# Latent attention: where the softmax rows are divided by their sums

## The chip, the cores and the metric

The kernel runs on one core of one Trainium2 chip. The metric is the device time of one launch in microseconds (us). The kernel before takes 4326.44 us, the median of three runs (4323.44 to 4328.68).

A core has five engines with an instruction queue each, and every queue is worked through in order: PE (TensorE, matrix products; PEld is its weight load), DVE (VectorE), ACT (ScalarE), POOL (GpSimd) and SP (SyncE, which here only issues transfers). An instruction that waits holds up all that is queued behind it on its engine.

## The reference

One layer of an encoder is applied to two groups of tokens, 256 ("prompt") and 1024 ("sample"), with the same weights. The layer is a mixer (retention beside latent attention), a cross-attention to 256 memory tokens, and a feed-forward part that picks experts by product keys. The change lies in the latent attention alone:

```python
def blk(qc):
    s = (einsum('bqhd,bkhd->bhqk', qc[..., :NOPE], k_nope)
         + einsum('bqhr,bkr->bhqk', qc[..., NOPE:], k_rope))
    p = softmax(s.astype(float32) * scale, axis=-1)
    return einsum('bhqk,bkhd->bqhd', p, v)
```

There are 8 heads with values 64 wide. For every query the output is the sum over the keys of exp(score) times value, divided by the sum of the exp.

## The kernel before

The program goes through these stages in order: the input projection and retention; the latent attention of the first group (256 tokens), whose work is mixed with the keys and values of the memory tokens; the first block of the rest of the layer; the latent attention of the second group (1024 tokens), at 829 to 1119 us of the profiled execution; the other two blocks; the gate tables; and a long dense expert stage. Nearly all products are made in three parts (`mm3`, L176: high by high, high by low, low by high), so a product of 512 columns is three matmuls.

The latent attention is `phase_m`. Its heads are taken two at a time ("a pair", `hp`, four of them). For a pair PE first makes the keys `kt` and the queries `qt`, which ACT and DVE split into a high and a low part. Then come the query tiles of 128 rows, 16 per pair in the second group: four (two heads by two tiles) make a batch, which shares one tile of transposed rows `pT` and one result `po`. The steps of a query tile are

- PE: the scores `sc` (called at L640, recorded under L179 to L181), six matmuls of 512 columns; there are two score buffers
- DVE: the row maximum (L642, recorded under L74)
- ACT: exp of the row into `pe`, with the sum of the row read out behind it (L644); there are two `pe` buffers
- DVE: the reciprocal of the sum, and a copy `r` of it across 64 columns (L646, L647, both under L74)
- PE: eight 128x128 transposes of `pe` (L657) into two PSUM tiles `tr` (there are two), and ACT copies each to `pT` (L658)

Once per batch, in `values`, PE lays the reciprocals out as rows by multiplying each `r` with the identity (L590, four products into the second half of `po`), makes the 16 products of the values with `pT` (L594, first half of `po`), and then ACT copies the second half to `ob` (L597), DVE multiplies the first half with it, ACT and DVE split the result into `oh`, and the ACT queue stores it to `mixT` (L602). `values` of a batch is called (`late`) when the next batch has its first tile under way. Matmuls on float32 data (L590, L594) run as two records each.

The order of the instructions on an engine is not the order of the code: a scheduler places them by its own model of time, and it does so for the whole program. DVE also carries work of later stages in between, a few instructions at a time: the routing of experts (L90) and products of gathered expert rows (`gj`, L90), each placed behind an instruction of the main line.

Of the kernel before, what the change touches and what calls it, by code (L numbers as in the profile page):

```python
# [10 lines left out]
F32 = mybir.dt.float32  # L11
# [4 lines left out]
AF = mybir.ActivationFunctionType  # L16
ALU = mybir.AluOpType
# [4 lines left out]
P = 128  # L22
# [37 lines left out]
def r32(ap):  # L60
    return ap.bitcast(F32)
# [46 lines left out]
class K:  # L108
# [423 lines left out]
    def phase_m(self, sd, g, lw):  # L532
        nc, tc, I = self.nc, self.tc, self.I
        v = self.v
        t0, nt = GROUPS[g]
        Tg = nt * P
        NB = min(Tg, 512)
        with ExitStack() as es:
# [4 lines left out]
            vs = ma.tile([P, nt, 512], F32, name=self.nm("vs"))  # L543
# [36 lines left out]
            po_ = es.enter_context(tc.tile_pool(name="mpo", bufs=1 + g, reuse_waits="tile", space=PSUM))  # L580
            ap = es.enter_context(tc.tile_pool(name="mb", bufs=1, reuse_waits="tile"))
            QG = 2 * P
            late = None

            def values(hp, q0, pTs, rs):

                po = po_.tile([P, 2, QG], F32, tag="po", name=self.nm("po"))
                for j in range(2):
                    for par in range(2):
                        nc.tensor.matmul(po[64 * par:64 * par + 64, 1, j * P:(j + 1) * P], rs[par][j], self.ident, start=True, stop=True)  # L590
                for j in range(nt):
                    for par in range(2):
                        h = 2 * hp + par
                        nc.tensor.matmul(po[64 * par:64 * par + 64, 0, :], vs[:, j, h * 64:(h + 1) * 64], pTs[par][j // 4][:, j % 4, :],  # L594
                                         start=j == 0, stop=j == nt - 1)
                ob = ap.tile([P, QG], F32, tag="ob", name=self.nm("ob"), bufs=2)
                nc.scalar.copy(ob, po[:, 1, :])  # L597
                v.tensor_tensor(ob, po[:, 0, :], ob, ALU.mult)
                oh = [ap.tile([P, QG], F32R, tag=f"oh{i}", name=self.nm("oh"), bufs=1) for i in range(2)]
                self.split(oh[0], oh[1], ob)  # L600
                for i in range(2):
                    nc.scalar.dma_start(sd["mixT"][g][i][:, hp, q0 * P:q0 * P + QG], r32(oh[i]))  # L602
                self.tick(0.1 * nt)

            for hp in range(MH // 2):
                S = kt
                for b in range(0, Tg, NB):
                    ps = pp.tile([P, 512], F32, tag="tr", name=self.nm("tr"))
                    bs = slice(b, b + NB)
                    for k in range(2):  # L610
                        w = [ukv[i][:, k, hp * 128:(hp + 1) * 128] for i in range(2)]
                        self.mm3(ps[:, :NB], w, (cT[0][:, 3 + k, bs], cT[1][:, 3 + k, bs]), k == 0, k == 1)
                    for par, r in ((0, slice(0, 64)), (1, slice(64, 128))):
                        self.split(S[par][0][r, bs], S[par][1][r, bs], ps[r, :NB])
                qts = []
                for par in range(2):
                    h = 2 * hp + par
                    qt = [ap.tile([P, Tg], F32R, tag=f"qt{g}{i}", name=self.nm("qt"), bufs=2) for i in range(2)]
                    for b in range(0, Tg, NB):
                        ps = pp.tile([P, 512], F32, tag="tr", name=self.nm("tr"))  # L620
                        bs = slice(b, b + NB)
                        for k in range(3):
                            self.mm3(ps[:, :NB], [uq[i][:, k, h, :] for i in range(2)], (cT[0][:, k, bs], cT[1][:, k, bs]), k == 0, k == 2)
                        qr = ap.tile([P, NB], F32, tag="qr", name=self.nm("qr"), bufs=1)
                        v.tensor_tensor(qr[:, :NB], ps[:, :NB], tq[par][:, bs], ALU.mult)
                        self.split(qt[0][:, bs], qt[1][:, bs], qr[:, :NB])
                    qts.append(qt)
                for q0 in range(0, nt, 2):
                    pTs, rs = [], []
                    for par in range(2):  # L630
                        qt = qts[par]
                        pT = [ap.tile([P, min(nt, 4), QG], F32, tag=f"pT{g}", name=self.nm("pT"), bufs=4) for _ in range(0, nt, 4)]
                        pTs.append(pT)
                        rs.append([])
                        for t in (q0, q0 + 1):
                            sl = slice(t * P, (t + 1) * P)
                            sp = psc.tile([P, max(Tg, 512)], F32, tag="sc", name=self.nm("sc"))
                            for b in range(0, Tg, NB):
                                bs = slice(b, b + NB)
                                self.mm3(sp[:, bs], (qt[0][:, sl], qt[1][:, sl]), (S[par][0][:, bs], S[par][1][:, bs]), True, True)  # L640
                            st = ap.tile([P, 2], F32, tag="st", name=self.nm("st"), bufs=4)
                            v.tensor_reduce(st[:, 0:1], sp[:, :Tg], AX.X, ALU.max, negate=True)  # L642
                            pe = ap.tile([P, Tg], F32, tag=f"pe{g}", name=self.nm("pe"), bufs=2)
                            nc.scalar.activation(pe[:, :Tg], sp[:, :Tg], AF.Exp, bias=st[:, 0:1], accum_out=st[:, 1:2])  # L644
                            r = ap.tile([P, 64], F32, tag="r64", name=self.nm("r64"), bufs=8)
                            v.reciprocal(st[:, 1:2], st[:, 1:2])  # L646
                            v.tensor_copy(r, st[:, 1:2].broadcast_to([P, 64]))  # L647
                            rs[par].append(r)
                            if late:
                                late()  # L650
                                late = None
                            self.tick(0.11 * nt)
                            for q in range(0, nt, 4):
                                n = min(4, nt - q)
                                ps = pp.tile([P, 512], F32, tag="tr", name=self.nm("tr"))
                                for j in range(n):
                                    nc.tensor.transpose(ps[:, j * P:(j + 1) * P], pe[:, (q + j) * P:(q + j + 1) * P], self.ident)  # L657
                                nc.scalar.copy(pT[q // 4][:, :, (t - q0) * P:(t - q0 + 1) * P], ps[:, :n * P].rearrange("p (a b) -> p a b", b=P))  # L658
                    late = lambda a=(hp, q0, pTs, rs): values(*a)
            late()  # L660


# [702 lines left out]
```

## Time and profile before

| what | us |
|---|---|
| median of three runs | 4326.44 |
| the profiled execution | 4333.59 |
| its span, first to last instruction | 4331.8 |
| PE busy in the span | 3994.1 |
| DVE busy | 3286.3 |
| ACT busy | 1633.1 |
| latent attention of the second group | 829 to 1119 |

A busy matmul is drawn from its start to its modelled end, and consecutive matmuls overlap; what one costs in a stream is read from start to start. The same holds for ACT, where an instruction begins before the one ahead has fully ended.

### The profile page before, as it was taken

The numbers are of one execution on the slowest core, as the hardware profiler recorded it, in microseconds if no ns is written. First come the engines' busy times: TensorE is split into PE (matmuls) and PEld (weight loads), VectorE is DVE, ScalarE is ACT, GpSimd is POOL, SyncE is SP. The second block draws the span as 40 slices with busy tenths as digits, with TensorE's granted clock in tenths as the row PEclk, the third lists the DMA queues.
The fourth block names the chain that finished last, engine by engine and source line by source line (L and its number), as shares of the span: only waits on it lengthen the run. The fifth ranks groups of instructions, "written<-read, shape, count | busy, mean of one in ns | idle before, by whom it ended". The sixth has DMA issues, their size and how long they took to land.

```text
span 4331.8 us, 66450 instructions
## 1 busy us (share of the span) xinstructions
PE 3994.1 (92%) x23202; PEld 3573.5 (82%) x23202; DVE 3286.3 (76%) x7044; ACT 1633.1 (38%) x3568; POOL 2277.9 (53%) x2090
## 2 busy tenths in 40 slices
PE   7999888899899899877899999999999999999997
PEld 7999877667588788766788888898888998888896
DVE  5556422687575697799799888888878788888888
ACT  6333534455443343689322222222222222222222
POOL 2221143012556401468456777776767767676775
PEclk9999999899999999999999999999999999999998
DMA  2112577324778648476876998898988888888887
GB/s 90 37 36 72 203 238 267 105 70 153 235 251 304 211 156 283 147 203 201 285 244 226 332 327 295 321 313 294 320 287 296 305 313 292 305 309 288 316 313 275
DMA packets 489008, 1030.74 MB, mean 238 GB/s; under 512 B 42720, under 2 KB 201952, under 8 KB 488672
## 3 DMA queue, kind: packets, MB, share of 16 engines
q0 software_dynamic: 149536, 545.33, 35.7%
q1 hardware_dynamic: 329200, 470.66, 33.0%
q10 hardware_dynamic: 9936, 10.51, 0.8%
q8 instruction: 182, 2.98, 0.3%
q14 instruction: 154, 1.26, 0.1%
HBM read 901.87 MB, written 124.45 MB: 237 GB/s over the span
## 4 chain that ended last, share of the span: by engine, by line
PE 45%; DVE 17%; issue 7%; DMA 5%; POOL 3%; ACT 2%; SPq 0%; another core or an unknown queue 0%; POOLq 0%; ACTq 0%; DVEq 0%
PE pa L181 6%; PE pa L179 6%; PE pa L180 6%; PE pv L180 5%; PE pv L181 5%; PE pv L179 5%; DVE o L74 4%; PE pj L179 2%; PE pj L181 2%; PE pj L180 2%; DVE gj L90 2%; DVE gps L90 2%; DMA ur<-in_uT 2%; POOL grow L1031 1%; DVE dacc L74 1%
## 5 line engine op out<-in xcount | busy, mean ns | idle before, releaser
L1031 POOL DMA_INDIRECT grow<-in_peer_u,gids x512 | 537.5, 1050 | 784.9 <-DVE gj L90 230.9
L179 PE MATMUL pa<-dxT,uh 128*128 128x384 f32 x2048 | 689.9, 337 | 18.4 <-ACT wr L1199 12.6
L1031 POOL DMA_INDIRECT grow<-in_peer_v,gids x512 | 513.5, 1003 | 350.9 <-DVE gps L90 201.6
L180 PE MATMUL pa<-dxT,uh 128*128 128x384 f32 x2048 | 689.8, 337 | 0.0
L181 PE MATMUL pa<-dxT,ul 128*128 128x384 f32 x2048 | 676.0, 337 | 0.4 <-POOL ul L1188 0.2
L90 DVE SCALAR_TENSOR_TENSOR gps<-grow,ga,gps 128x1024 f32<-128x1024 f32 x512 | 656.5, 1282 | 14.0 <-DMA grow<-in_peer_v,gids 6.2
L179 PE MATMUL pv<-vh,wh 128*128 128x512 f32 x1536 | 605.7, 398 | 44.4 <-DVE dacc L74 39.7
L180 PE MATMUL pv<-vl,wh 128*128 128x512 f32 x1536 | 610.7, 398 | 8.3 <-POOL vl L1216 8.2
L181 PE MATMUL pv<-vh,wl 128*128 128x512 f32 x1536 | 609.3, 397 | 1.8 <-DVE wl L74 1.8
L90 DVE SCALAR_TENSOR_TENSOR gj<-grow,gps 128x1024 bf16<-128x1024 f32 x384 | 466.5, 1215 | 7.9 <-ACT gps L1058 1.6
L74 DVE TENSOR_TENSOR dacc<-pv,dacc 128x1024 f32<-128x1024 f32 x258 | 311.9, 1218 | 152.8 <-PE pv L181 142.1
L212 POOL TENSOR_TENSOR wl<-wraw,wh 128x512 fp32r<-128x512 f32 x180 | 240.2, 1352 | 343.1 <-ACT wh L208 253.4
L179 PEld LDWEIGHTS pa<-dxT,uh 128*128 128x128 f32 x2048 | 386.8, 189 | 33.5 <-ACT wr L1199 14.0
L181 PEld LDWEIGHTS pa<-dxT,ul 128*128 128x128 f32 x2048 | 385.6, 189 | 10.9 <-POOL ul L1188 4.4
L180 PEld LDWEIGHTS pa<-dxT,uh 128*128 128x128 f32 x2048 | 386.8, 189 | 6.4
L179 PEld LDWEIGHTS pv<-vh,wh 128*128 128x128 f32 x1536 | 293.5, 191 | 110.6 <-DVE dacc L74 48.4
L1187 ACT CAST uh<-ur 128x512 fp32r<-128x512 f32 x256 | 158.6, 621 | 584.8 <-DMA ur<-in_uT 539.2
L1188 POOL TENSOR_TENSOR ul<-ur,uh 128x512 fp32r<-128x512 f32 x256 | 333.3, 1306 | 65.1 <-ACT uh L1187 59.1
L1216 POOL TENSOR_TENSOR vl<-vr,vh 128x512 fp32r<-128x512 f32 x256 | 333.2, 1320 | 59.7 <-ACT vh L1215 56.6
L180 PEld LDWEIGHTS pv<-vl,wh 128*128 128x128 f32 x1536 | 293.8, 191 | 66.8 <-POOL vl L1216 12.3
L181 PEld LDWEIGHTS pv<-vh,wl 128*128 128x128 f32 x1536 | 293.3, 191 | 59.3 <-DVE wl L74 2.8
L179 PE MATMUL pj<-act,wh 128*128 128x256 f32 x1088 | 311.1, 295 | 22.4 <-ACT act L173 7.5
(285 smaller groups left out, 9077.6 us busy)
## 6 DMA issues: line engine op xcount, KB each, us to landing
ur<-in_uT SPq DMA_DIRECT2D x256, 256.0 KB
vr<-in_peer_v SPq DMA_DIRECT2D x256, 256.0 KB
G<-st SPq DMA_DIRECT2D x96, 512.0 KB
gt<-G SPq DMA_DIRECT2D x64, 768.0 KB
wraw<-in_peer_wq SPq DMA_DIRECT2D x96, 256.0 KB
wraw<-in_w_out SPq DMA_DIRECT2D x48, 256.0 KB
wraw<-in_ca_wq SPq DMA_DIRECT2D x48, 256.0 KB
x<-ld SPq DMA_DIRECT2D x24, 512.0 KB
```

The costliest lines, as they stand in the source:

```text
L74: r = f(*a, **kw)
L90: r = f(*a, **kw)
L179: mm(ps, a[0], b[0], start=first, stop=False)
L180: mm(ps, a[0], b[1], start=False, stop=False)
L181: self.mm = mm(ps, a[1], b[0], start=False, stop=last).ins
L212: (nc.vector if self.spare and k in self.spare else eng).tensor_tensor(wl[:, :n], raw[:, :n], r32(wh[:, :n]), ALU.subtract)
L1031: nc.gpsimd.indirect_dma_start(out=u, out_offset=None, in_=src, in_offset=bass.IndirectOffsetOnAxis(ap=ids[:, s:s + 1], axis=0))
L1187: nc.scalar.copy(uh, ur)
L1188: nc.gpsimd.tensor_tensor(ul, ur, r32(uh), ALU.subtract)
L1216: nc.gpsimd.tensor_tensor(vl, vr, r32(vh), ALU.subtract)
```

## The change

Each row of exp is multiplied with the reciprocal of its sum on ACT, in place in `pe`, before it is transposed. The tile `r`, its copy on DVE, the products with the identity on PE, the copy to `ob` and the product on DVE are left out, and `po` has one half only; `oh` is split from `po` directly. In the second group that is 64 more ACT instructions of 128x1024, and in the first 16 of 128x256.

```diff
-            def values(hp, q0, pTs, rs):
+            def values(hp, q0, pTs):
-                po = po_.tile([P, 2, QG], F32, tag="po", name=self.nm("po"))
-                for j in range(2):
-                    for par in range(2):
-                        nc.tensor.matmul(po[64 * par:64 * par + 64, 1, j * P:(j + 1) * P], rs[par][j], self.ident, start=True, stop=True)
+                po = po_.tile([P, QG], F32, tag="po", name=self.nm("po"))
...
-                ob = ap.tile([P, QG], F32, tag="ob", name=self.nm("ob"), bufs=2)
-                nc.scalar.copy(ob, po[:, 1, :])
-                v.tensor_tensor(ob, po[:, 0, :], ob, ALU.mult)
-                self.split(oh[0], oh[1], ob)
+                self.split(oh[0], oh[1], po)
...
-                            r = ap.tile([P, 64], F32, tag="r64", name=self.nm("r64"), bufs=8)
                             v.reciprocal(st[:, 1:2], st[:, 1:2])
-                            v.tensor_copy(r, st[:, 1:2].broadcast_to([P, 64]))
-                            rs[par].append(r)
+                            nc.scalar.activation(pe[:, :Tg], pe[:, :Tg], AF.Copy, scale=st[:, 1:2])
```

How ACT's order changes is seen in the middle of a pair of heads of the second group. Before, with `tr` the transposed quarters of a row and `sc` the scores:

```order
L644 ACTIVATE pe_12295,st_12293<-sc_12282,st_12293 128x1024
L658 COPY pT_12251<-tr_12276 128x4x128
L658 COPY pT_12250<-tr_12300 128x4x128
L644 ACTIVATE pe_12323,st_12321<-sc_12314,st_12321 128x1024
L658 COPY pT_12251<-tr_12306 128x4x128
L644 ACTIVATE pe_12383,st_12381<-sc_12374,st_12381 128x1024
L658 COPY pT_12312<-tr_12362 128x4x128
L597 COPY ob_12349<-po_12328 128x256
```

And of the change (L637 is the exp, L639 the new multiplication, L649 the copy):

```order
L637 ACTIVATE pe_11568,st_11566<-sc_11559,st_11566 128x1024
L649 COPY pT_11474<-tr_11545 128x4x128
L649 COPY pT_11475<-tr_11551 128x4x128
L637 ACTIVATE pe_11597,st_11595<-sc_11588,st_11595 128x1024
L639 ACTIVATE pe_11568<-pe_11568,st_11566 128x1024
L639 ACTIVATE pe_11597<-pe_11597,st_11595 128x1024
L649 COPY pT_11557<-tr_11576 128x4x128
L649 COPY pT_11558<-tr_11582 128x4x128
```

Query tiles now go through ACT two by two: both multiplications stand behind the second exp and ahead of the copies.

PE's order at the same place before, where a score product is followed by the transposes of one tile (each `x4` is four transposes) and a product for the sums:

```order
L181 MATMUL sc_12432<-kt_9497,qt_12125 128x512
L590 MATMUL po_12482<-c_ident,r_2541_12325 64x128
L657 MATMUL tr_12392<-c_ident,pe_12383 128x128 x4
L657 MATMUL tr_12398<-c_ident,pe_12383 128x128 x4
L179 MATMUL sc_12464<-kt_9495,qt_12090 128x512
```

And of the change (L648 is the transpose, L591 the product of the values; the score `sc_11559` is complete ahead of these rows, and 13 more value products of the same kind stand between the first two pieces):

```order
L181 MATMUL sc_11559<-kt_9453,qt_11298 128x512
L591 MATMUL po_11493<-pT_11418,vs_9455 64x256
L591 MATMUL po_11493<-pT_11335,vs_9455 64x256
...
L181 MATMUL sc_11588<-kt_9453,qt_11298 128x512
L648 MATMUL tr_11516<-c_ident,pe_11489 128x128 x4
L648 MATMUL tr_11522<-c_ident,pe_11489 128x128 x4
L648 MATMUL tr_11545<-c_ident,pe_11541 128x128 x4
L648 MATMUL tr_11551<-c_ident,pe_11541 128x128 x4
L179 MATMUL sc_11615<-kt_9451,qt_11263 128x512
```

The transposes of two tiles now stand together, behind the scores of the next two tiles, and in every second such group 15 value products stand between those two scores.

## Rows read from the trace of the kernel before

**Rows 1.** The page: span, and busy time of each engine.

```profile
span 4331.8 us, 66450 instructions
PE 3994.1 (92%) x23202; PEld 3573.5 (82%) x23202; DVE 3286.3 (76%) x7044; ACT 1633.1 (38%) x3568; POOL 2277.9 (53%) x2090
```

**Rows 2.** Windows, second group's attention: from:to, length, busy per engine, PE clock, DMA.

```profile
829.00:900.00 71.00, 65.11 (x393) 45.47 (x393) 60.87 (x255) 41.25 (x77) 2.92 (x3) 0.95 0.15 49
900.00:966.00 66.00, 60.92 (x365) 44.99 (x365) 62.80 (x228) 38.21 (x72) 3.13 (x3) 0.97 0.14 44
966.00:1038.00 72.00, 69.88 (x431) 50.19 (x428) 53.03 (x106) 42.48 (x81) 19.14 (x17) 1.00 0.46 140
1038.00:1110.00 72.00, 69.36 (x431) 50.26 (x428) 52.33 (x103) 42.45 (x80) 18.91 (x17) 1.00 0.57 182
```

**Rows 3.** Timeline of ACT, exps at a pair's ends: start, us, instruction.

```profile
1037.88 1.13 ACT L644 ACTIVATE pe<-sc,st 128x1024 f32<-128x1024 f32 x1
1057.79 1.12 ACT L644 ACTIVATE pe<-sc,st 128x1024 f32<-128x1024 f32 x1 [0.51 <-DVE st L74]
1110.59 1.12 ACT L644 ACTIVATE pe<-sc,st 128x1024 f32<-128x1024 f32 x1
```

**Rows 4.** Timeline of PE inside the last pair.

```profile
1067.59 0.44 PE L590 MATMUL po<-c_ident,r 128*64 128x128 f32 x4
1067.96 0.66 PE L657 MATMUL tr<-c_ident,pe 128*128 128x128 f32 x4
1068.37 0.48 PE L179 MATMUL sc<-kt,qt 128*128 128x512 f32 x1
...
1069.85 0.60 PE L657 MATMUL tr<-c_ident,pe 128*128 128x128 f32 x4
...
1072.88 3.62 PE L594 MATMUL po<-pT,vs 128*64 128x256 f32 x31
```

**Rows 5.** Timeline of ACT inside the last pair.

```profile
1069.38 1.11 ACT L644 ACTIVATE pe<-sc,st 128x1024 f32<-128x1024 f32 x1
1070.39 0.19 ACT L644 ACTIVATION_READ_ACCUMULATOR pe<-sc,st 128x1 f32 x1
1070.49 0.59 ACT L658 COPY pT<-tr 128x512 f32<-128x512 f32 x1
...
1079.47 0.59 ACT L658 COPY pT<-tr 128x512 f32<-128x512 f32 x1 [0.31 <-PE tr L657]
...
1079.96 0.59 ACT L658 COPY pT<-tr 128x512 f32<-128x512 f32 x1
```

**Rows 6.** Line groups, 820 to 1120 us: xcount, busy us, mean ns, idle before.

```profile
L590 PE MATMUL po<-c_ident,r 128*64 128x128 f32 x128 | 20.4, 297 | 1.4 <-DVE r L74 1.2
L74 DVE TENSOR_REDUCE st<-sc 128x1 f32<-128x1024 f32 x64 | 77.7, 1216 | 15.2 <-PE sc L181 14.7
L644 ACT ACTIVATE pe<-sc,st 128x1024 f32<-128x1024 f32 x64 | 72.0, 1125 | 14.2 <-DVE st L74 10.1 <-DVE sel L90 1.7 <-DVE r L74 1.7
L597 ACT COPY ob<-po 128x256 f32<-128x256 f32 x16 | 6.0, 372 | 27.8 <-PE po L594 27.7
```

**Rows 7.** Lines 822 and 826, the memory attention's exp and multiplication: ns min/median/max.

```profile
L822 ACT ACTIVATE pe<-s,st x40: 462/475/587, 659.4 to 1585.9; 128x256 f32<-128x256 f32 x40
L826 ACT ACTIVATE pe<-pe,st x40: 491/508/581, 661.4 to 1590.2; 128x256 f32<-128x256 f32 x40
```

**Rows 8.** Windows, after a wait of PE on DVE between two pairs.

```profile
900.00:904.00 4.00, 0.81 (x2) 0.74 (x3) 3.89 (x18) 0.98 (x2) 0.00 (x0) 0.87 0.10 33
904.00:908.00 4.00, 4.00 (x14) 3.11 (x14) 2.61 (x8) 0.87 (x2) 0.00 (x0) 0.70 0.36 98
```

**Rows 9.** Windows, the first group's attention and the stretch behind it.

```profile
480.00:590.00 110.00, 110.00 (x731) 96.44 (x730) 40.67 (x103) 47.94 (x119) 27.79 (x22) 1.00 0.56 184
590.00:630.00 40.00, 27.15 (x113) 20.94 (x112) 11.35 (x17) 14.21 (x27) 15.50 (x13) 0.87 0.89 309
```

More of the change, by code (lines that the diff above doesn't have):

```diff
@@ L593, in values @@
                         h = 2 * hp + par
-                        nc.tensor.matmul(po[64 * par:64 * par + 64, 0, :], vs[:, j, h * 64:(h + 1) * 64], pTs[par][j // 4][:, j % 4, :],
+                        nc.tensor.matmul(po[64 * par:64 * par + 64, :], vs[:, j, h * 64:(h + 1) * 64], pTs[par][j // 4][:, j % 4, :],
                                          start=j == 0, stop=j == nt - 1)
-                ob = ap.tile([P, QG], F32, tag="ob", name=self.nm("ob"), bufs=2)
-                nc.scalar.copy(ob, po[:, 1, :])
-                v.tensor_tensor(ob, po[:, 0, :], ob, ALU.mult)
                 oh = [ap.tile([P, QG], F32R, tag=f"oh{i}", name=self.nm("oh"), bufs=1) for i in range(2)]
-                self.split(oh[0], oh[1], ob)
+                self.split(oh[0], oh[1], po)
                 for i in range(2):
@@ L628, in phase_m @@
                 for q0 in range(0, nt, 2):
-                    pTs, rs = [], []
+                    pTs = []
                     for par in range(2):
@@ L633, in phase_m @@
                         pTs.append(pT)
-                        rs.append([])
                         for t in (q0, q0 + 1):
@@ L658, in phase_m @@
                                 nc.scalar.copy(pT[q // 4][:, :, (t - q0) * P:(t - q0 + 1) * P], ps[:, :n * P].rearrange("p (a b) -> p a b", b=P))
-                    late = lambda a=(hp, q0, pTs, rs): values(*a)
+                    late = lambda a=(hp, q0, pTs): values(*a)
             late()
```

## The prediction, made before the changed kernel was run

> **What bounds the kernel now.** I read the page first: PE is busy 3994 of 4332 us and ACT 1633 [rows 1], so over the whole kernel PE is short and ACT has room. That average decides nothing here, since the change lies in two stretches only. The windows come next. In the second group's attention PE is busy 69.9 and 69.4 of 72 us in the later two stretches, ACT 42.5, DVE 53 and 52 [rows 2]. In the first two DVE is nearly as full as PE (60.9 of 71 and 62.8 of 66), because it carries routing in between. So PE sets the pace in the later half, and PE and DVE by turns in the first.
>
> The third view is the timeline of ACT, for the pace. In the last pair the first exp starts at 1057.79 and the last at 1110.59: 52.8 us for 15 tile steps, 3.52 us a tile or 14.1 us a batch of four. From the last exp of a pair to the first of the next it is 19.9 us (1037.88 to 1057.79) [rows 3]: that is where PE makes the next keys and queries.
>
> The fourth view is the timeline of PE inside that pair, for costs from start to start [rows 4]. Four transposes take 0.41 us (1067.96 to 1068.37), so a tile's eight take 0.82; the six score matmuls take 1.48 (1068.37 to 1069.85); four records of the products with the identity take 0.37 (1067.59 to 1067.96), so the eight of a batch take 0.74; 31 records of the value products take 3.62, so the 32 of a batch take 3.74. A batch on PE is 4 x (1.48 + 0.82) + 3.74 + 0.74 = 13.7 us of the 14.1: PE is the bound by start-to-start costs too.
>
> ACT from start to start [rows 5]: exp with its readout 1.11 (1069.38 to 1070.49), a copy 0.49 (1079.47 to 1079.96). With `ob` and the split of `oh` at 0.37 each (the latter taken at the former's row [rows 6]), a batch is 4 x 1.11 + 8 x 0.49 + 0.74 = 9.1 us.
>
> **What is removed.** On PE 128 records in the second group [rows 6], 0.74 us a batch: its floor falls to 12.9 us. On ACT `ob`, 0.37 us a batch. On DVE the copy `r` and the product into `ob`; in the later two stretches DVE waits anyway, so I count nothing, and in the first two they go into the allowance below.
>
> **What is added.** The trace has no ACT multiplication of 1024 columns. The nearest row is the same operation on 256 columns, 508 ns. An exp takes 475 ns at 256 columns [rows 7] and 1125 at 1024 [rows 6], 0.85 ns a column, so 508 + 768 x 0.85 = 1.16 us, and 1.06 from start to start, since consecutive ACT instructions overlap by 0.10 (a copy is 0.59 long and the next starts 0.49 later). From below it is bounded by the 0.51 of the narrow row, from above by an exp with its whole readout, 1.12 + 0.19 = 1.31. I take 1.06, from the same operation carried to the width. ACT's batch is then 9.1 - 0.37 + 4 x 1.06 = 13.0 us.
>
> **How the two fit together.** Neither floor, 12.9 or 13.0, is above 14.1. But the queues are worked in order, there are two score buffers and two `pe` buffers, and the new order takes tiles two by two: ACT does both multiplications, two copies of the first tile, an exp, two copies of the second, an exp. Without a wait that is 2.12 + 0.98 + 1.11 + 0.98 + 1.11 = 6.3 us. Half of these double steps can run like that. In the other half the first copy waits for PE: a score product (1.48) that cannot start before the exp ahead has freed its buffer, 2.0 us before the double step begins; then 15 value products (30 records, 3.5); the second score product (1.48); four transposes and their release (0.41 + 0.15). Its sum is 7.0, less 2.0, so the copy starts at 5.0 where ACT was done at 2.5, and the step ends at 5.0 + 4.2 = 9.2. A batch is 6.3 + 9.2 = 15.5 us against 14.1. The added wait is ACT's for PE, and behind it in ACT's queue stands the exp that frees the score buffer for which PE waits next: they take turns where PE ran through. The loss is 1.4 us a batch, 3.75 batches between first and last exp, four pairs: **+21 us**. If the multiplication took 0.51, the short step would shrink to 5.2, the batch to 14.4, and the loss to 4; with 1.31 it would be 16.0, and 29.
>
> Between two pairs, the last tiles wait for two multiplications (2.1 us) before their transposes, and PE then has the same projections and fewer products (0.74). Counted through, that is 20.2 us against 19.9: **+1 us** over four pairs, 0 to +8.
>
> In that place PE stands idle: it has transposed the tiles ahead some 1.7 us before the last exp starts, and can go on 2.3 us after that start, a hole of 4.0 us. The trace has such a hole: with PE busy only 0.81 of 4 us, the granted clock is 0.87 in that stretch and 0.70 in the next [rows 8], which makes (0.13 + 0.30) x 4 / 0.5 = 3.4 us at the lower of the two levels, 1.2 GHz, and costs 1.7 us of PE's work. I count half of four such losses: **+3 us**, 0 to +7.
>
> In the first two pairs, waits on DVE leave PE idle for 6 of 71 and 5 of 66 us [rows 2]; a slower loop overlaps some of that, and DVE has less to do: **-4 us**, 0 to -8.
>
> In the first group PE is busy 110 of 110 us with the memory's products mixed in, and ACT 48 [rows 9]. PE loses 32 records, 3 us; ACT gains 16 narrow multiplications of 0.41, 6.6 us, which its 62 idle us cover, and PE has other products to do meanwhile. Without that cover they would cost up to 6.6 and end at +4. In the 40 us behind, PE is busy 27 and the DMA engines 0.89 of the time, so a part of the gain is waited away: **-2 us**, -3 to +4.
>
> The scheduler also shifts single instructions in later stages. No row prices this; I take 0, and as bounds the 8 us that a measurement can barely tell. The stages behind the second group start when its buffers come free, so they move with it.
>
> The sum is 21 + 1 + 3 - 4 - 2 = +19 us. The profiled execution took 4333.6 us (span 4331.8 and 1.8 around it), 7.2 above the median of the runs; against its own time the change gives 4352.6, and for the median 4326.4 + 19 = **4345 us**.
>
> **The rivals.** *ACT's work is hidden.* If exps, copies and transposes overlapped better than my count, both floors would fit under 14.1, the loops would stay at their pace, and only the first group's 2 us would be gained: 4324 us. For it speaks ACT's 42.5 of 72; against it that 13.0 of 14.1 leaves 1.1 us for all waits of a batch, and one of them is 2.5.
>
> *PE's relief decides.* If PE stayed the bound, a batch would take its 12.9 us plus the 0.4 that it loses now: 0.74 x 3.75 x 4 = 11 us less in the loops, 3 in the gaps between pairs, 3 in the first group: 4309 us, faster. It needs ACT to stay ahead of PE by the whole length of the value products; only the stretches of PE at 97% speak for that.
>
> *The lower clock spreads.* If the clock fell in each gap between pairs and stayed low for its 20 us, PE would lose 10 us a pair instead of the 0.85 counted: 4345 + 4 x 9 = 4382 us. Against it speaks [rows 8], where it was back after 3.4 us, and the clock of 1.00 in both later stretches [rows 2]. The Trainium skill, "TensorE: Matmul & The Clock Gate", section "Part 4: PE-mode transpose", says that transposes do not count as PE work for the clock in the way that other products do; by that rule the double transposes, which now stand next to the holes, would make this rival likelier. The trace does not bear it out so far: transposes are 0.82 of 3.4 us of every tile, at the full 2.4 GHz.
>
> **How the numbers follow.** My forecast has 62%, with 4336 to 4362 as its own range; hidden work 20%; PE's relief 10%; the clock 8%. Under 0.2%, 8.7 us, a measurement of this kernel can't tell a change from none, so "same" is 4317.8 to 4335.1. Faster is the relief and a little of the hidden case: 0.12. Same is most of the hidden case and the lowest edge of mine: 0.20. Slower is 0.68. The range from 4318 to 4368 leaves out the relief below and the clock's case above; the cheapest multiplication (4328) and the dearest (4353) lie inside it.
>
> **What would show it.** Right: in the last pair some 58 us from first to last exp instead of 52.8; exps that follow one another in a short and a long rhythm; ACT busy about 58 of 72 us; waits of ACT's copies on PE's transposes and of PE's scores on ACT's exp that are new, in total some 2.5 us a batch; a multiplication of 1.16 us. Wrong: a batch that keeps to 14.1 us or falls below it, PE still busy 97%, or a loss that lies outside 829 to 1119 us.

## The result and the profile after

The changed kernel takes 4349.53 us, the median of seven runs (4339.22 to 4358.74), beside 4327.33 us for the kernel before in seven runs on the same chip: a ratio of 1.0052, 95% interval 1.0037 to 1.0067, or 22 us slower. The prediction was 4345 us, range 4318 to 4368, slower with a chance of 0.68.

The page of the changed kernel, its span and the busy time of each engine, beside [rows 1]:

```profile
span 4354.3 us, 66114 instructions
...
PE 3996.1 (92%) x23042; PEld 3565.8 (82%) x23042; DVE 3270.9 (75%) x6944; ACT 1696.5 (39%) x3628; POOL 2273.0 (52%) x2090
```

PE lost 160 records and is busy 2 us longer: part of it ran at the lower clock (below). The span is 22.5 us longer. From the first exp of the second group to the end of its last value product it was 286.4 us (830.9 to 1117.3) and is 313.9 (822.7 to 1136.6), 27.5 more. The group begins 8.2 us earlier, and what stands behind it takes 3.2 us more; in the fourteen traces of this document that part is 3204 to 3232 us long, so only the 27.5 is read further.

The windows of the second group, beside [rows 2]:

```profile
829.00:900.00 71.00, 60.48 (x347) 41.41 (x346) 57.40 (x235) 50.69 (x83) 2.92 (x3) 0.95 0.17 52
900.00:966.00 66.00, 58.44 (x331) 41.04 (x329) 59.43 (x196) 49.78 (x81) 5.45 (x5) 1.00 0.15 44
966.00:1038.00 72.00, 65.11 (x351) 46.64 (x352) 43.74 (x74) 51.94 (x84) 16.90 (x16) 0.95 0.43 132
1038.00:1110.00 72.00, 64.64 (x367) 46.19 (x364) 45.39 (x75) 50.22 (x81) 16.72 (x15) 0.98 0.50 164
```

In every window PE is less busy than before (64.6 where it was 69.4), DVE too, and ACT is busier by 8 to 12 us but never full. No engine is the bound any more: they take turns. How, the timeline of ACT in the last pair shows, a short double step and then a long one (start, length, instruction, and in brackets the idle time ahead with what ended it):

```profile
1091.49 1.13 ACT L637 ACTIVATE pe<-sc,st 128x1024 f32<-128x1024 f32 x1
...
1092.59 1.08 ACT L649 COPY pT<-tr 128x512 f32<-128x512 f32 x2
1093.53 1.16 ACT L637 ACTIVATE pe<-sc,st 128x1024 f32<-128x1024 f32 x1
...
1094.63 2.31 ACT L639 ACTIVATE pe<-pe,st 128x1024 f32<-128x1024 f32 x2
1097.07 1.07 ACT L649 COPY pT<-tr 128x512 f32<-128x512 f32 x2
1098.03 1.13 ACT L637 ACTIVATE pe<-sc,st 128x1024 f32<-128x1024 f32 x1
...
1099.13 1.08 ACT L649 COPY pT<-tr 128x512 f32<-128x512 f32 x2
1100.07 1.16 ACT L637 ACTIVATE pe<-sc,st 128x1024 f32<-128x1024 f32 x1
...
1101.17 2.30 ACT L639 ACTIVATE pe<-pe,st 128x1024 f32<-128x1024 f32 x2
1104.60 0.37 ACT L170 CAST oh<-po 128x256 fp32r<-128x256 f32 x1 [1.12 <-PE po L591]
...
1106.64 1.08 ACT L649 COPY pT<-tr 128x512 f32<-128x512 f32 x2 [1.67 <-PE tr L648]
1107.60 1.13 ACT L637 ACTIVATE pe<-sc,st 128x1024 f32<-128x1024 f32 x1
```

The exps start 2.04, 4.50, 2.04 and 7.53 us apart: a double step of 6.5 and one of 9.6, a batch of 16.1 (the expectations below round it to 16.0). The long one on PE:

```profile
1099.30 0.50 PE L179 MATMUL sc<-kt,qt 128*128 128x512 f32 x1 [0.45 <-ACT pe L637]
...
1100.89 3.67 PE L591 MATMUL po<-pT,vs 128*64 128x256 f32 x30
1104.49 0.50 PE L179 MATMUL sc<-kt,qt 128*128 128x512 f32 x1
...
1106.01 1.03 PE L648 MATMUL tr<-c_ident,pe 128*128 128x128 f32 x8
```

The exp of 1107.60 writes into the `pe` buffer of the exp of 1098.03, the one but one ahead of it. That buffer is free when PE has transposed its row (1106.01), which waits behind the value products, and ACT reaches that exp only behind the copies of 1106.64.

What PE waited for in the second group (total us, times, longest), in the kernel before:

```profile
PE tr L657 <- ACT pe L644: 6.6, 5, 4.5
PE tr L179 <- DVE kt L74: 3.9, 1, 3.9
PE sc L179 <- ACT pe L644: 3.0, 7, 0.7
PE tr L657 <- ACT pT L658: 2.6, 8, 0.6
```

and in the changed one:

```profile
PE sc L179 <- ACT pe L637: 13.8, 26, 2.5
PE tr L648 <- ACT pe L639: 10.7, 6, 2.0
PE tr L648 <- ACT pT L649: 10.2, 27, 1.3
PE po L591 <- ACT pT L649: 3.7, 4, 0.9
```

The waits for ACT that are shown add up to 12.2 us before and 38.4 after, while PE's waits for DVE fell from 5.1 to 2.3 us: all of the growth is PE waiting for ACT.

### The profile page after: what moved, and what is told of

It is laid out like the page before. It is cut to its first block, busy times and chain, and to the rows that moved or that the text cites. A ratio compares the mean times of both kernels' runs of the same rounds, so it can differ in the third digit from the quotient of the medians.

```text
span 4354.3 us, 66114 instructions
## 1 busy us (share of the span) xinstructions
PE 3996.1 (92%) x23042; PEld 3565.8 (82%) x23042; DVE 3270.9 (75%) x6944; ACT 1696.5 (39%) x3628; POOL 2273.0 (52%) x2090
## 4 chain that ended last, share of the span: by engine, by line
PE 53%; DVE 20%; DMA 9%; issue 9%; ACT 5%; POOL 4%; SPq 0%; POOLq 0%; ACTq 0%; DVEq 0%
PE pa L181 5%; PE pa L179 5%; PE pa L180 5%; PE pj L179 5%; PE pj L180 5%; PE pj L181 5%; PE pv L180 5%; PE pv L179 5%; PE pv L181 5%; DVE o L74 4%; DVE gps L90 3%; DMA ur<-in_uT 2%; DVE gj L90 2%; DVE oh L90 1%; DVE dacc L74 1%
## 5 line engine op out<-in xcount | busy, mean ns | idle before, releaser
L180 PEld LDWEIGHTS pv<-vl,wh 128*128 128x128 f32 x1536 | 295.4, 192 | 67.1 <-POOL vl L1207 12.6
```

What stands on the lines that cost most here:

```text
L180: mm(ps, a[0], b[1], start=False, stop=False)
```

## The experiments

The theory at the outset: a row now visits ACT twice, ACT's queue is in order, and PE and ACT take turns; neither engine's work is too much by itself. Rivals: ACT's added work, the duration of the multiplication, the two-by-two order of the tiles, the lump of value products. The table gives for each run the median, the ratio to the kernel before on the same chip with its 95% interval, and, worked out from the starts of the exps in the trace, the sum of the four loops (first to last exp of a pair) and the sum of the three gaps between pairs and the tail behind the last exp, in us. The ratio is not that of the medians in the table, since each run has its own runs of the kernel before beside it. Loops, gaps and tail come from one execution each: the second group is the same code in "before" and "first group only", and there the loops differ by 2.8 us and gaps and tail by 1.0. The expectations name some runs by labels: e1 is the multiplication taken out, e2 the spare multiplication, e8 half of each row.

| kernel | median | ratio | loops | gaps, tail |
|---|---|---|---|---|
| before | 4327.33 | 1 | 212.9 | 73.5 |
| changed | 4349.53 | 1.0052 (1.0037 to 1.0067) | 231.4 | 82.5 |
| no multiplication | 4319.14 | 0.9977 (0.9964 to 0.9991) | 201.4 | 70.4 |
| before + spare multiplication | 4340.09 | 1.0016 (1.0002 to 1.0030) | 213.0 | 81.8 |
| half of each row | 4341.15 | 1.0040 (1.0023 to 1.0056) | 226.7 | 76.6 |
| multiplication on DVE | 4358.81 | 1.0059 (1.0039 to 1.0079) | 226.6 | 81.7 |
| values in two lumps | 4381.83 | 1.0123 (1.0106 to 1.0140) | 264.2 | 81.2 |
| one tile at a time | 4381.15 | 1.0119 (1.0101 to 1.0137) | 261.0 | 80.1 |
| three exp buffers | 4325.52 | 0.9994 (0.9983 to 1.0006) | 205.0 | 79.7 |
| filled hole | 4354.23 | 1.0062 (1.0043 to 1.0081) | 231.6 | 76.3 |
| first group only | 4324.20 | 0.9983 (0.9971 to 0.9994) | 210.1 | 72.5 |
| before, sums transposed | 4325.81 | 0.9991 (0.9980 to 1.0003) | 207.3 | 70.1 |
| both of these | 4323.79 | 0.9987 (0.9975 to 0.9999) | 208.7 | 70.5 |
| both, three exp buffers | 4330.45 | 1.0014 (1.0002 to 1.0026) | 208.8 | 77.4 |

### The multiplication taken out

```diff
-                            nc.scalar.activation(pe[:, :Tg], pe[:, :Tg], AF.Copy, scale=st[:, 1:2])
```

> The changed kernel with the multiplication of the rows left out (so the division by the sums is left out), everything else as changed: no products with the identity, no `ob`. My theory (the multiplication stands between exp and transposes in ACT's queue and makes ACT and PE take turns; PE's relief is real but unused) expects the batch of four tiles to fall from 16.0 us to PE's floor of 12.9 to 13.4, the long and short double steps to go, PE at over 95% in 966 to 1038 us, and 4305 to 4318 us in all. A rival, that PE's products with the identity were free (hidden in other waits), expects the batch of before, 14.1 us, and some 4324 us.

The loops fall to 201.4, 11.5 below the kernel before. So what the change removes is worth something, and the change's +18.5 in the loops is -11.5 of relief and 30.0 that come with the multiplication. The median of 4319 us lies 1 us above the range expected.

### The multiplication off the chain

To the kernel before, the same multiplication is added on ACT; its result goes to a spare buffer that nothing reads.

```diff
+                            spare = ap.tile([P, Tg], BF, tag=f"spare{g}", name=self.nm("spare"), bufs=1)
+                            nc.scalar.activation(spare, pe[:, :Tg], AF.Copy, scale=st[:, 1:2])
```

> The kernel before, with an ACT multiplication of each row added that nothing waits for: same input, same width, same scale, its result (bf16) goes to a spare tile. The division stays where it was. My theory, that the place in the chain costs and not the ACT time, expects at most a quarter of the change's loss in the second group: a batch of 14.1 to 14.6 us and 4325 to 4335 us, ACT busy 60 of 72 us. The rival, that ACT's time is what costs (ACT is full), expects a batch near 16 us and 4345 to 4355 us.

Its line group and its last window (as in [rows 6] and [rows 2]):

```profile
L650 ACT ACTIVATE spare<-pe,st 128x1024 bf16<-128x1024 f32 x64 | 74.6, 1166 | 1.6 <-DVE st L74 0.9
```

```profile
1038.00:1110.00 72.00, 68.39 (x420) 48.91 (x420) 51.89 (x101) 56.08 (x92) 18.76 (x17) 1.00 0.57 183
```

ACT is 13.6 us busier than before in that window, and the loops keep their length (213.0 for 212.9). ACT's load alone costs nothing there, and neither does a second visit of the row to ACT, as long as the transposes do not wait for it. In gaps and tail it costs 8.3 us, about what the changed kernel loses there, and the median of 4340 us is above the 4325 to 4335 expected.

### The multiplication on DVE

The row is still multiplied between exp and transposes, but on an engine where exp does not queue.

```diff
-                            nc.scalar.activation(pe[:, :Tg], pe[:, :Tg], AF.Copy, scale=st[:, 1:2])
+                            v.tensor_scalar(pe[:, :Tg], pe[:, :Tg], st[:, 1:2], None, ALU.mult)
```

> The changed kernel with the multiplication of the rows on DVE instead of ACT, same place in the chain. In its order exps and copies follow one another tile by tile again. If the order two by two is the cause, the loops where DVE has room (the last two pairs) come back to 13.5 to 14.5 us a batch, and only the first two pairs, where DVE is full, lose: 4325 to 4350 us. If one more step in the chain costs on any engine, the last two pairs keep 15.5 to 16 us a batch and the whole takes 4350 us or more. The width of an f32 row on DVE is not priced by the trace: between 0.4 and 1.3 us.

Windows of the first and the last stretch:

```profile
829.00:900.00 71.00, 58.90 (x336) 40.61 (x335) 62.11 (x245) 35.92 (x68) 3.18 (x3) 0.93 0.15 45
...
1038.00:1110.00 72.00, 66.28 (x388) 48.44 (x386) 58.06 (x94) 40.03 (x74) 17.12 (x16) 0.98 0.55 173
```

The loops of the four pairs are 60.3, 60.3, 52.4 and 53.6. The last two, where DVE has room, are as long as before the change (52.2 and 52.8), but that hides PE's relief: without any multiplication they are 49.5 and 50.6. Beside these the step costs 3 us a loop on DVE, where on ACT it costs 7.5 and 6.4. So the longer chain by itself is less than half of the cost. The rest is not the place in ACT's queue alone, since DVE's multiplication is also shorter (0.75 us against 1.17). In the first two pairs the loops are 5 to 8 us longer than before; that DVE's routing work is the reason is not shown by a run. The median of 4359 us is above the 4325 to 4350 of the theory.

### Half of each row

Only the first half of each row is multiplied.

```diff
-                            nc.scalar.activation(pe[:, :Tg], pe[:, :Tg], AF.Copy, scale=st[:, 1:2])
+                            nc.scalar.activation(pe[:, :Tg // 2], pe[:, :Tg // 2], AF.Copy, scale=st[:, 1:2])
```

> The changed kernel with only the first half of each row multiplied (half of the division is left out): 0.6 instead of 1.15 us an instruction. My theory says that the long double step (9.5 us) is set by PE's chain of scores, value products, scores and transposes and so keeps its length, and only the short one (6.5) shrinks by two half multiplications, 1.1 us, to 5.4: a batch of 14.9 to 15.2 us and 4335 to 4341 us. The rival, that ACT's load sets the pace, expects both steps to shrink by 1.1: a batch of 13.9 us and 4322 to 4328 us.

ACT in a short double step:

```profile
1091.03 1.16 ACT L637 ACTIVATE pe<-sc,st 128x1024 f32<-128x1024 f32 x1
...
1092.13 0.76 ACT L639 ACTIVATE pe<-pe,st 128x512 f32<-128x512 f32 x1
1093.28 0.72 ACT L639 ACTIVATE pe<-pe,st 128x512 f32<-128x512 f32 x1 [0.40 <-DVE st L74]
1094.55 1.07 ACT L649 COPY pT<-tr 128x512 f32<-128x512 f32 x2 [0.54 <-PE tr L648]
1095.51 1.13 ACT L637 ACTIVATE pe<-sc,st 128x1024 f32<-128x1024 f32 x1
```

The saved time turns into waits, for the reciprocal and then for the transposes; exp to exp it is 4.5 us as with whole rows. A double step of 6.5 and one of 9.3 make a batch of 15.8, where 14.9 to 15.2 were expected, and the loops fall by 4.7 of the 30.0 us that come with the multiplication. The duration is the smaller part of the cost.

### The value products in two lumps

If the long step is long because of the 30 records that stand in PE's queue, two lumps of half the size, one head each, change the rhythm.

```diff
-                for j in range(nt):
-                    for par in range(2):
+                for par in range(2):
+                    for j in range(nt):
...
+                    if par == 0:
+                        yield
```

> The changed kernel with a batch's 16 value products issued in two lumps of 8, one head's ahead of the next batch's first tile and the other's ahead of its third; same products, same multiplications. My theory (ACT waits for the lump of value products between two scores) expects the short and long double steps to give way to two of 7.4 to 7.8 us: a batch of 14.9 to 15.5 us instead of 16.0, 8 to 16 us less than the change in all, 4335 to 4343 us. The rival, that ACT's load or the plain latency of one more step costs, expects the batch to stay at 16 us and the time at 4349 us.

All double steps become long, 2.0 + 7.5 = 9.5 us, a batch of 19.1 where 14.9 to 15.5 were expected. The lump sets the step, but the halves did not get shorter. In the gaps between pairs the same products stand free; here in the changed kernel, 16 records that alternate between the heads,

```profile
1053.71 1.95 PE L591 MATMUL po<-pT,vs 128*64 128x256 f32 x16
```

and here 8 records of one head:

```profile
1081.87 1.94 PE L591 MATMUL po<-pT,vs 128*64 128x256 f32 x8
```

Products of the two heads write to two halves of 64 columns of PE and run side by side when they alternate. The Trainium skill, "TensorEngine Tiling (Array Packing)", section "Tiling Modes", says that tiles operate independently and can execute in parallel; the trace agrees, at 0.12 us a record against 0.24. So the run tells nothing on shorter lumps.

### One tile at a time

The same instructions, with an order forced on PE and ACT: exp of a tile behind the multiplication of the one ahead, and that multiplication behind the copies ahead of it.

```diff
+                            if self.mul is not None:
+                                self.pace(m1, self.mul)
...
+                            if self.copied is not None:
+                                self.pace(m2, self.copied)
```

> The changed kernel with its instructions unchanged and their order held tile by tile: an exp stands behind the multiplication of the tile before, a multiplication behind the copies of the tile before, and the scores of a tile behind the transposes of the tile two before. What e1, e2 and e8 showed (ACT's load costs nothing in the loops, half the multiplication saves little) leaves the order as the cause: the scheduler puts tiles two by two once the multiplication stands between exp and transposes. This theory expects a batch of 13.2 to 14.1 us instead of 16.0, loops of 49 to 53 us, and 4315 to 4332 us. The rival, that one more step between exp and transposes with two buffers costs in any order, expects a batch of 15.5 us or more and 4345 us or more.

PE's waits in the second group:

```profile
PE tr L662 <- ACT pe L650: 67.3, 45, 4.9
```

The loops grow to 261.0, with transposes waiting 67.3 us for the multiplication. A part of that is the clock, which is at 1.2 GHz for 21.9 us of these loops and for 3.4 us of the changed kernel's. The theory of this run is refuted: with these buffers the order two by two is better than this one.

### Three exp buffers

```diff
-                            pe = ap.tile([P, Tg], F32, tag=f"pe{g}", name=self.nm("pe"), bufs=2)
+                            pe = ap.tile([P, Tg], F32, tag=f"pe{g}", name=self.nm("pe"), bufs=3)
```

> The changed kernel with three buffers for the exp rows instead of two. Theory of the buffers: with two of them an exp cannot start before both tiles ahead are multiplied and transposed, and that forces the turn-taking; with a third, a batch goes from 16.0 us to 13.5 to 14.5, the loops of a pair (first to last exp) from 58 to about 52 us, and the kernel comes to 4325 to 4338 us. Rival, that the multiplication's place in ACT's queue behind the exp and ahead of the copies costs the turn whatever the buffers: the batch stays at 16 us, the loops at 57 to 59, the kernel at 4344 to 4354.

ACT in the last pair:

```profile
1074.37 1.14 ACT L637 ACTIVATE pe<-sc,st 128x1024 f32<-128x1024 f32 x1
...
1075.47 1.16 ACT L639 ACTIVATE pe<-pe,st 128x1024 f32<-128x1024 f32 x1
1076.51 1.08 ACT L649 COPY pT<-tr 128x512 f32<-128x512 f32 x2
1077.45 1.16 ACT L637 ACTIVATE pe<-sc,st 128x1024 f32<-128x1024 f32 x1
...
1078.55 1.18 ACT L639 ACTIVATE pe<-pe,st 128x1024 f32<-128x1024 f32 x1
```

PE at the same place, the transposes of the row whose multiplication starts at 1075.47:

```profile
1078.02 1.04 PE L648 MATMUL tr<-c_ident,pe 128*128 128x128 f32 x8
```

PE's waits:

```profile
PE sc L179 <- ACT pe L637: 10.8, 12, 2.9
PE tr L648 <- ACT pT L649: 4.9, 11, 0.9
...
PE tr L648 <- ACT pe L639: 2.6, 3, 0.9
```

Exps follow one another in 2.1 to 3.1 us, with one step of 5.5 to 6.0 a batch, and a batch is 13.8 us; the loops fall from 231.4 to 205.0, 3.6 above those without any multiplication. This one number takes back 26.4 of the 30.0 us: with a third buffer the kernel is level with the one before. The rows show the buffer in use: the exp of 1077.45 starts while the row two ahead of it waits for its transposes (1078.02). With two buffers it would have had to wait for their end, as the exp of 1107.60 does in the changed kernel. So most of the multiplication's cost in the loops goes with having two buffers, where an exp cannot start until the row two ahead has been multiplied and transposed. The third buffer also brings another order: tiles go one at a time, each multiplication behind the exp of the next tile. The run before forced a different one, with the exp behind the multiplication of the tile ahead. The new order with two buffers was not run, so the share of the order alone stays open.

The Trainium skill, "Perfetto Trace Analysis", section "Optimization Strategy", says that the same gap, repeated on the engine that should be saturated, can mean too few buffers for the next tile. The trace agrees: a wait such as the 0.45 us ahead of a score product comes back all through the changed kernel's second group, 26 times and 13.8 us in all, and with the third buffer 12 are left, though these are longer (10.8 us).

### The hole between pairs filled

To the changed kernel, six products of the identity with values (12 records) are added once per pair, into a half of a result buffer that nothing reads, behind the transposes of the third-last tile.

```diff
+                            if g and q0 == nt - 2 and par == 1 and t == q0 + 1:
+                                for j in range(6):
+                                    self.pace(nc.tensor.matmul(self.po[:, 1, :], self.ident, vs[:, j, 0:QG], start=True, stop=True), self.tr[-3])
```

> The changed kernel with twelve more matmul records per pair (six products of the identity with values, into a half of a result buffer that nothing reads), placed behind the transposes of the third-last tile of a pair, where PE stands idle. Theory, that the idle places between pairs let the granted clock fall to 1.2 GHz and that this makes the gaps longer: the clock stays at full there, each gap is 1.5 to 3 us shorter than 25.7, 23.4, 22.4 and the tail 10.9, and the kernel is 5 to 9 us faster than the changed one, 4340 to 4345 us. Rival, that the clock falls for another reason or that the gap is set by ACT's two multiplications alone: the gaps keep their length or grow by up to 1 us each, 4349 to 4354 us.

Windows around the gap behind the third pair in the changed kernel (the last figures are the granted clock, the DMA share and GB/s):

```profile
1046.00:1050.00 4.00, 2.02 (x10) 1.50 (x10) 0.97 (x3) 4.00 (x6) 2.55 (x2) 0.86 0.64 209
1050.00:1054.00 4.00, 4.00 (x20) 2.86 (x20) 0.00 (x0) 2.04 (x5) 0.00 (x0) 0.71 0.43 158
```

and with the hole filled:

```profile
1046.00:1050.00 4.00, 3.76 (x26) 3.18 (x25) 4.00 (x7) 3.21 (x7) 1.65 (x2) 1.00 0.52 136
1050.00:1054.00 4.00, 3.20 (x19) 2.10 (x18) 0.48 (x3) 4.00 (x6) 2.05 (x2) 1.00 0.66 206
```

The clock keeps 2.4 GHz through all three gaps, the gaps shrink from 25.7, 23.4 and 22.4 to 23.8, 21.8 and 21.8 us and the tail from 10.9 to 8.8, 6.2 in all, though 12 records a pair came on top. So the lower clock does lengthen the gaps. It is not the only thing that does: with three exp buffers no gap has the lower clock, and gaps and tail are still 79.7 us, 6.2 more than before the change. The median, expected at 4340 to 4345 us, does not show it: at 1.0062 (1.0043 to 1.0081) beside 1.0052 (1.0037 to 1.0067) the two cannot be told apart, and whether the 6 us reach the end of the kernel stays open.

### The change in the first group alone

The second group keeps the code of before; an `if not g` in the loop and in `values` picks the one or the other.

```diff
+                            if not g:
+                                nc.scalar.activation(pe[:, :Tg], pe[:, :Tg], AF.Copy, scale=st[:, 1:2])
+                            else:
```

> The change in the first group (256 tokens) alone; the second group as before. In the profile of the changed kernel the second group began 8 us earlier than before. If that is the first group's gain (PE is full there and loses 32 records, 3 us, the rest from a better order), this kernel takes 4318 to 4325 us, 3 to 10 less than before. If it was only the order of the block in between, it lies within 3 us of before.

0.9983 (0.9971 to 0.9994), 5.6 us faster by the medians. Where the time is saved its trace does not tell: the second group starts at 832.0 us, later than before, and its loops and gaps, whose code is that of before, are 3.8 us shorter. In all traces with a changed first group the second one starts at 820.8 to 832.0 us, in the other three at 827.8 to 830.9, so the spread is as large as the gain.

### The sums by one transpose, without the multiplication

To the kernel before: the reciprocals of two heads stand side by side, and one 128x128 transpose per query tile lays both out, two records a batch instead of eight.

```diff
-                    for par in range(2):
-                        nc.tensor.matmul(po[64 * par:64 * par + 64, 1, j * P:(j + 1) * P], rs[par][j], self.ident, start=True, stop=True)
+                    nc.tensor.transpose(po[:, 1, j * P:(j + 1) * P], rs[j].rearrange("p a b -> p (a b)"), self.ident)
```

> The kernel before with cheaper products for the sums: the reciprocals of both heads of a query tile lie side by side in one 128x128 tile, and one transpose per query tile lays them out, two records a batch instead of eight. PE's theory (PE bounds the loops of the kernel before, e1 gave back 2 us a loop and 15 in all in the second group) expects a batch some 0.5 us shorter, 7 to 9 us in the second group and 1 to 2 in the first: 4315 to 4322 us against some 4328. The rival, that these products lie in waits, expects 4326 to 4330 us.

The loops fall by 5.6 and gaps and tail by 3.4. This is half of what leaving the multiplication out saved in the loops (11.5), for no work on ACT. The median falls by 4 us, to 4326 where 4315 to 4322 were expected, and its interval just includes no change.

### Both gains together

The first group of the one and the second group of the other, no other edit.

> The first group as in the changed kernel (rows divided on ACT), the second as before but with its sums laid out by one transpose of a whole tile per query tile instead of four products with the identity. Theory, that the two gains seen apart (first group -5.6 us, transposed sums -3.0 us) belong to separate stretches and add up: -8 to -9 us, 4317 to 4322 us, ratio .9975 to .9985. Rival, that the order of later stages, which the scheduler sets anew in every version, gives and takes as much: anything within 4318 to 4332 us.

4323.79 us, 0.9987 (0.9975 to 0.9999): faster than both kernels, by a little. By the median it is no faster than the first group's part alone, and lies in the rival's range and not in the theory's. But the two ratios seen apart, 0.9983 and 0.9991, have intervals of 0.0012 to either side, and so has this one: whether the two gains add up stays open. In its trace the second group is 279.2 us long, 7.2 less than before.

### A third exp buffer without the multiplication

To this last kernel the third buffer is added, the control on the experiment that decided; for room the tile of the sums has three buffers instead of four.

```diff
-                            pe = ap.tile([P, Tg], F32, tag=f"pe{g}", name=self.nm("pe"), bufs=2)
+                            pe = ap.tile([P, Tg], F32, tag=f"pe{g}", name=self.nm("pe"), bufs=2 + g)
```

> The kernel with the first group's rows divided on ACT and the second group's sums laid out by one transpose per query tile, now with three buffers for the second group's exp rows (and three instead of four for the tile of the sums). A control on the third buffer: the second group has no multiplication here. Theory, that the third buffer heals only the second visit of a row to ACT: the loops of a pair stay at 50 to 55 us, as with two buffers (51.9, 55.3, 50.7, 50.8), and the kernel within 5 us of 4324. Rival, that a third buffer speeds up any version, so that it says nothing on the multiplication: the loops shorten by 2 to 5 us each here too, and the kernel comes to 4304 to 4316 us.

The loops are 208.8, with two buffers 208.7. A third buffer is worth nothing in the loops where no multiplication stands between exp and transposes, and 26 us where one does. Gaps and tail are 6.9 us longer and the kernel with them, 4330 us where at most 4329 were expected; why was not tried.

## Why the prediction was right, step by step

- *The loops, +21.* Measured +18.5. The mechanism was right: the short and the long double step were to be 6.3 and 9.2 us, a batch 15.5; they are 6.5, 9.6 and 16.1. A loop grew by 4.2 to 5.3 us and not by 3.75 x 2.0 = 7.5, since only three of its steps are the long 7.5.
- *What sets the size.* The prediction named the order of the queues and the two `pe` buffers together and did not part them. The third buffer shows that with only two they take turns; it changes the order as well, so the order's own share stays open. And the loss was tied to the length of the multiplication, 14.4 us a batch at 0.51 us. That step failed: at 0.72 us (0.62 from start to start), where by the same arithmetic the batch is some 14.6, it is 15.8.
- *PE's relief* was a rival with 11 us in the loops. Its size was right to half a us (11.5), as the run without the multiplication shows; in the changed kernel the turns hide it.
- *Between pairs, +1, and the lower clock, +3.* Measured +9.0, the term that was mis-sized; how the 20.2 us between two pairs were counted, the prediction does not show. The hole behind the third pair has 2.9 us of idle time (0.92 + 1.98) where 4.0 were forecast:

```profile
1045.99 0.65 PE L591 MATMUL po<-pT,vs 128*64 128x256 f32 x2 [0.92 <-ACT pT L649]
1048.62 3.51 PE L648 MATMUL tr<-c_ident,pe 128*128 128x128 f32 x16 [1.98 <-ACT pe L639]
```

  But the lower clock lasts longer: 6.8, 6.8, 3.4 and 6.8 us from 885, 967, 1049 and 1127 on, where 3.4 was counted in half of the pairs. The first of them in windows:

```profile
884.00:888.00 4.00, 2.31 (x13) 1.91 (x14) 2.99 (x21) 2.47 (x4) 0.00 (x0) 0.64 0.09 32
888.00:892.00 4.00, 4.00 (x13) 2.73 (x13) 0.67 (x5) 1.35 (x3) 0.00 (x0) 0.51 0.00 0
```

  The clock misses 0.36 and 0.49 of 4 us, at half speed (0.36 + 0.49) x 4 / 0.5 = 6.8 us. All four, 23.8 us, are 11.9 us of PE's work; 3.4 us of the lower clock stood in the gaps before the change as well [rows 8]. The filled hole won back 6.2 of the 9.0. What the remaining 2.8 are was not taken apart.
- *First two pairs, -4.* Not there: their loops grew by 4.2 and 5.3, the others by 4.8 and 4.2. The 11 us in which PE was idle there were put down to DVE, but its waits for DVE itself are 5.1 us in the whole group.
- *The first group, -2.* About -6, from the run of that part alone (-2.6 to -12.6 by its interval), not located in the trace. The misses offset each other: in the second group 27.5 where 21 + 1 + 3 - 4 = 21 were forecast, ahead of it -6 where -2 was, and 22 us came out where 19 were forecast. That the sum lies nearer than its terms is luck.
- *The multiplication, 1.16 us.* Its line group, beside the narrow one of [rows 7]:

```profile
L639 ACT ACTIVATE pe<-pe,st 128x1024 f32<-128x1024 f32 x64 | 73.8, 1165 | 5.9 <-DVE st L74 5.8
```

- *What would show it.* Loops of 58 us: 57.0 to 59.4. The rhythm and PE's waits on exp: there. ACT busy 58 of 72 us: 50 to 52; the 58 were the work of a pair, and a pair with its gap now takes 79 us, not 72. Copies that wait for transposes were to be new; they waited before as well (25.7 us, now 17.7), at no cost while ACT had slack.
- *The lower clock spreads* (the rival at 4382): no. It fell in each gap and was back after at most 6.8 us.

## What to carry to other kernels

A step added to an engine that is 59% busy can cost loop time when the engine already works on the same row earlier and the next engine waits for the new step: the row's buffer is then held for two passes through one in-order queue, one behind the other, and for what follows them. Count the buffers against the steps that a row now makes before its buffer is free, and try one more buffer before judging the change. Judge engine load and chain separately: here the load alone cost nothing in the loops, the step on an engine with room 3 us a loop, and both together some 7.

## What the runs showed of the hardware

- Alternating products on two halves of 64 columns of PE take 0.12 us a record of 256 columns, one half alone 0.24.
- In the changed kernel PE's idle places of 2.9 us in a gap (0.92 + 1.98 us, 0.65 of work between them) went with 3.4 to 6.8 us at 1.2 GHz; with 2.8 us of filler in them the clock stayed at 2.4 GHz.
- The same multiplication of 128x1024 takes 0.75 us on DVE (mean of 64) and 1.17 on ACT.
